# Seeding a product's PSUM bank with ScalarE, and one down word earlier, in a two-layer macaron encoder

## The chip, the cores and the metric

The kernel runs on one core of one Trainium2 chip. TensorE multiplies, ScalarE, VectorE and GpSimd work on tiles beside it, SyncE issues most of the loads from HBM. The metric is the device time of one execution in microseconds (us), the median of three runs. A profile of one further execution shows every instruction of every engine.

## The reference

The input x has 256 tokens of 1024 features, all in float32. Two layers each do three steps, and each step ends in a layer norm of the old x, scaled, plus the step's result: a SwiGLU feed-forward, a mixer (layer 0 a bidirectional mLSTM, layer 1 a windowed attention), and a second SwiGLU feed-forward. What this change touches is the feed-forward, which is done four times:

```python
gu = x @ w_in                          # (256, 1024) @ (1024, 5632)
g, u = gu[..., :2816], gu[..., 2816:]
return (silu(g) * u) @ w_out           # (256, 2816) @ (2816, 1024)
```

## The kernel before, in words

**Three matmuls for one.** A float32 product is computed to nearly full precision by splitting each operand into a high part (rounded to the type that TensorE takes in one pass) and a low part (what the rounding left). `mm3` (line 617) then issues high by high, high by low and low by high into the same PSUM bank. ScalarE casts the high part, VectorE subtracts to get the low part. This holds for weights (tiles `w_raw`, `s_raw` to `w_hi`, `w_lo`), for x (`xT_hi`, `xT_lo`) and for the hidden activations (`h_hi`, `h_lo`). A piece of weights of 128 x 1024 is called a word.

**A feed-forward** (`ffn`, line 770). Its 2816 hidden columns are done as 512 plain columns, 256 plain columns and four blocks of 512. Each of the four blocks is one call of `seven` (line 946): it gets the four 128-token by 512-column results (two token tiles t, gate and up) with seven products in place of eight, a Strassen-Winograd scheme over sums of weights and sums of x (`S1` to `S4`). One call of `product` (line 930) takes two words and issues 12 matmuls of 512 columns.

**Order of work in a block.** The products go to PSUM banks qa, qb and qc, of a ring of four banks `pw` that `wbank` gives out; each product's follow-up on the other engines is a function `end1` to `end7` that is issued right behind it. In issue order:

1. product 1 into qa; `end1` (line 955) has ScalarE copy qa to an SBUF tile `e` (the page calls all these temporaries `e` or `g`).
2. `before()`: for the first block it transposes the 256 plain columns (`turn`, line 1033); for the second to fourth block it is `second` (line 1002) of the block before, which transposes that block's result for token tile 1 with `tr` (line 790): four TensorE transposes into one bank, ScalarE casts the bank to `h_hi`, VectorE subtracts to `h_lo` (`split_evac`, line 636).
3. product 2 into qc; `end2` (line 958) asks VectorE to add qc onto `e`. The sum is the gate of token tile 0.
4. `down(1)` (line 914): one word of w_out times one 128-column chunk of the hidden activations, added onto the four `py` banks of the output. For each token tile it issues six matmuls, tile 0 first, then tile 1. Chunks are taken in order: the first block's first `down` reads chunk 2 of the plain columns; the first `down` of the second, third and fourth block reads chunk 6, 10 and 14, which is the first chunk of the block before. Its token tile 0 was transposed near the end of that block (`end4`, line 977), its token tile 1 by the `second` of step 2. The order of h in `mm3` is high, high, low: the third matmul of each three loads `h_lo`.
5. products with S1 (into qb; `end5` copies it) and S2 (onto qa; `end6` copies it and has ScalarE do the SiLU of `e` in place), a second `down`, products with S3 and S4, and so on. The first three blocks do four `down`, the last block two; six more follow in `tail`.

**What sets the order on the other engines.** All engines execute their own instructions in the order in which they were issued. The kernel writes that order with a planner of its own: class `Paced` (line 65) keeps a clock for TensorE, VectorE and ScalarE while the program is written out, adding a cost for each instruction (`on_tensor`, line 162). After every matmul or transpose, `Weights.fill` (line 376) hands ScalarE another cast of a weight word (`high`, line 300) if ScalarE's clock is less than 300 ns ahead of TensorE's, and VectorE a subtraction (`low`, line 324), a sum of weights (`sum`) or a deferred follow-up (`when_ready`, line 365), by the same rule. `flush` (line 372) issues all deferred follow-ups at once; `down` calls it first. The words are listed in `plan` in the order in which the products use them (`seven` at line 492 of the planning code), and loads follow that list; a ring of ten split words lies between the splitting and TensorE.

Of the kernel before, what the change touches and what calls it, by code (L numbers as in the profile page):

```python
# [11 lines left out]
AF = mybir.ActivationFunctionType  # L12
# [52 lines left out]
class Paced:  # L65
# [94 lines left out]
            self.mark(o, self.act + 125)  # L160

    def on_tensor(self, name, n, out, ins):
        self.pe = max(self.pe, self.when(*ins)) + (109.0 if name == "transpose" else n / 2.4 + 13.3)
        for o in out:
            self.mark(o, self.pe + 200)
        if self.filler is not None:
            self.filler()
# [277 lines left out]
def trunk_kernel(ctx: ExitStack, tc: tile.TileContext, x, ffn_w_in, ffn_w_out, ln_g, ln_b, ml_w_in, ml_gate_b,  # L445
                 ml_norm_g, ml_w_out, at_w_in, at_sink, at_w_out, out):
    nc = Paced(tc.nc)
# [12 lines left out]
    def word(src, k, tag="w_raw"):  # L460
        words.append(dict(src=src, k=k, tag=tag))
        return len(words) - 1
# [3 lines left out]
    def split_of(w, scale=None, needs=None, takes=2720.0, behind=0.0):  # L466

        plan.append(dict(word=w, k=words[w]["k"], scale=scale, needs=needs, due=clock[0], behind=behind))
        clock[0] += takes
        return len(plan) - 1  # L470

    def piece(src, k, scale=None, takes=2720.0):
        split_of(word(src, k), scale, None, takes)

    def two(w, r0, c0):
        return w[r0:r0 + 256, c0:c0 + 512].rearrange("(k p) f -> p k f", p=128)
# [12 lines left out]
    def rows(w, c, scale=None):  # L489
        piece(w[c * 128:(c + 1) * 128, :].rearrange("(k p) f -> p k f", p=128), 1, scale)  # L490

    def seven(w, c0, c1, n, down):

        def at(r0, c):
            return [two(w, r0 + 256 * j, c) for j in range(2)]

        b12, b11, b22 = ([word(x, 2, TAGS[r]) for x in at(*p)]
                         for r, p in ((2, (0, c1)), (4 if n % 2 else 1, (0, c0)), (3, (512, c1))))
        b21 = at(512, c0)
        full = n < SEVENS - 1  # L500
        half = 1360.0
        s1 = [split_of(w_, None, None, half) for w_ in b11]
        for j in range(2):
            after[s1[j]] = [(b11[j], b12[j]), (b12[j], at(512, c1)[j])]
        for a in b21:
            piece(a, 2, None, half)
        down(1)
        t1 = [split_of(w_, None, p, half, BY_SUM) for w_, p in zip(b11, s1)]
        for j in range(2):
            after[t1[j]] = [(b11[j], b22[j])]  # L510
        t2 = [split_of(w_, None, p, half, BY_SUM) for w_, p in zip(b11, t1)]
        for j in range(2):
            after[t2[j]] = [(b11[j], b21[j])]
        down(1)
        for w_, p in zip(b12, s1):
            split_of(w_, None, p, half, BY_MOVE)
        for w_ in b22:
            split_of(w_, None, None, half)
        if full:
            down(1)  # L520
        for w_, p in zip(b11, t2):
            split_of(w_, None, p, half, BY_MOVE)
        if full:
            down(1)

    ends = {}
    for j, (kind, l, i, _) in enumerate(stages):
        if kind == "ffn":
# [3 lines left out]
            def down(n):  # L532
                for _ in range(n):
                    rows(wo, next(nth))
# [48 lines left out]
    W = Weights(nc, wpool, rooms, words, plan, after)  # L583
# [9 lines left out]
    ident = consts.tile([128, 128], F32, name="ident")  # L593
# [2 lines left out]
    nc.vector.tensor_scalar(ident, ji, 0.0, None, op0=OP.is_equal)  # L596
    mhalf = consts.tile([128, 2], F32, name="mhalf")
    nc.gpsimd.memset(mhalf, -0.5)

    gcol = consts.tile([128, 8], F32, name="gcol")  # L600
    gw = consts.tile([128, 8, 16], F32, name="gw")
# [20 lines left out]
    def pair(p, *idx):  # L622
        return p[0][idx], p[1][idx]

    def wbank(shape=(128, 512)):
        return psum.tile(list(shape), F32, name="pw", tag="pw", bufs=4)

    def ybank(shape=(128, 512)):
        return psum.tile(list(shape), F32, name="py", tag="py", bufs=4)
# [3 lines left out]
    def tok(t):  # L633
        return slice(t * 128, (t + 1) * 128)
# [135 lines left out]
    def ffn(l, i, n, pending, last):  # L770
        with ExitStack() as ph:
# [7 lines left out]
            def temp(name):  # L779
                return pool.tile([128, 512], F32, name=name, tag="t", bufs=6)  # L780

            start = pending is None
# [7 lines left out]
            def tr(hB, t, h):  # L790
                p = wbank((128, 4, 128))
                for k in range(4):
                    nc.tensor.transpose(p[:, k], h[:, k * 128:(k + 1) * 128], ident)
                split_evac(pair(hB, A, A, tok(t)), p, wait=True)

            def chunks(hB, n_):
                c0 = len(hT)
                for c in range(n_):
                    hT[c0 + c] = pair(hB, A, c)
# [114 lines left out]
            def down(n_):  # L914
                if not y:
                    y.extend([ybank() for _ in range(2)] for _ in range(2))
                W.flush()
                for _ in range(n_):
                    c = done_[0]
                    w, = W.take(1)  # L920
                    for t in range(2):
                        for o in range(2):
                            mm3(y[t][o], pair(hT[c], A, tok(t)), pair(w, A, 0, slice(o * 512, o * 512 + 512)),
                                c == 0, False)
                    W.done()
                    done_[0] += 1
# [3 lines left out]
            def product(bank, x_of, first, then):  # L930

                for j in range(2):
                    w, = W.take(1)
                    for k in range(2):
                        mm3(bank, x_of(2 * j + k), pair(w, A, k), first and j == k == 0, j == k == 1, not first)
                then()
                W.done()

            def copied(bank, name):
                e = temp(name)  # L940
                nc.scalar.copy(e, bank)
                return e
# [3 lines left out]
            def seven(full, before):  # L946

                of = lambda k0, t: (lambda k: pair(xT, A, k0 + k, tok(t)))
                sum_ = lambda name: (lambda k: pair(xs[name], A, k))
                v = {}  # L950
                hB = h_room(4)
                chunks(hB, 4)
                qa, qc = wbank(), wbank()

                def end1():
                    v["g0"] = copied(qa, "e1")

                def end2():
                    W.when_ready(lambda: nc.vector.tensor_add(v["g0"], v["g0"], qc), qc)

                def end5():
                    v["u1"] = copied(qb, "e5")

                def end6():
                    v["u0"] = copied(qa, "e2")
                    W.flush()
                    nc.scalar.activation(v["g0"], v["g0"], AF.Silu)

                def end7():
                    W.when_ready(lambda: nc.vector.tensor_sub(v["u1"], v["u1"], qa), qa)  # L970

                def end3():
                    W.flush()
                    W.when_ready(lambda: nc.vector.tensor_sub(v["u0"], qb, v["u0"]), qb)
                    W.when_ready(lambda: nc.vector.tensor_mul(v["u0"], v["g0"], v["u0"]))

                def end4():
                    v["g1"] = temp("g1")
                    nc.scalar.activation(v["g1"], qa, AF.Silu)
                    W.flush()  # L980
                    tr(hB, 0, v["u0"])
                    W.when_ready(lambda: nc.vector.tensor_mul(v["u1"], v["g1"], v["u1"]), v["g1"])

                product(qa, of(0, 0), True, end1)
                before()
                if not full:
                    gb.extend(load_ln(lambda name: W.room(name, TAGS[1]), l, n))
                product(qc, of(4, 0), True, end2)
                down(1)
                qb = wbank()  # L990
                product(qb, sum_("S1"), True, end5)
                product(qa, sum_("S2"), False, end6)
                down(1)
                product(qa, sum_("S3"), False, end7)
                product(qb, sum_("S4"), False, end3)
                if full:
                    down(1)
                product(qa, of(4, 1), False, end4)
                if full:
                    down(1)  # L1000

                def second():
                    W.flush()
                    tr(hB, 1, v["u1"])

                return second
# [16 lines left out]
            hh = []  # L1023
# [9 lines left out]
            def turn():  # L1033
                p = wbank((128, 2, S))
                for t in range(2):
                    for k in range(2):
                        nc.tensor.transpose(p[:, k, tok(t)], hh[t][:, k * 128:(k + 1) * 128], ident)
                split_evac(hp, p, wait=True)

            down(1)  # L1040
# [595 lines left out]
```

## Time and profile before

| what | value |
|---|---|
| runs | 914.19, 912.9 and 914.21 us, median 914.19 us |
| the profiled execution | span 911.7 us from its first to its last instruction; no time of its own is given beside the span |
| granted TensorE clock | 0.999 |
| TensorE matmuls | 902.5 us busy, 4459 instructions |
| VectorE | 804.4 us busy, 971 instructions |
| ScalarE | 573.1 us busy, 793 instructions |
| GpSimd | 152.5 us busy, 192 instructions |
| HBM read | 206.65 MB |

The page lists the engines as PE (TensorE's matmuls), PEld (its weight loads, which overlap with the matmuls), DVE (VectorE), ACT (ScalarE) and POOL (GpSimd). A row of a group reads: line, engine, operation, output <- inputs, shapes, count, then the busy time in us and the mean ns of one. Nearly all instructions bear line 180, since a wrapper there records them, so they are told apart by their tiles. A row of the timeline reads: start in us, duration in us, engine, operation, and in square brackets how long the engine had been idle before it and on whom it waited. Successive instructions of one engine can overlap by some 0.1 us in the rows, since a row ends when the result is written and the next one has started by then. Matmul rows overlap more (a row of 0.39 us every 0.23 us).

### The profile page before, as it was taken

What the parts mean: (1) busy time and instruction counts of PE and PEld (TensorE: products, weight loads), DVE (VectorE), ACT (ScalarE), POOL (GpSimd) and SP (SyncE); (2) the same over time, 40 slices, a digit from 0 to 9 for tenths busy, and PEclk for the clock granted to TensorE, in tenths of its full rate; (3) what the DMA queues carried; (4) which work ended last, traced back from release to release, by engine and by line L of the source; (5) the groups of instructions that cost most, each with busy time, mean ns of one, the idle gap of its engine ahead of it and who ended that gap; (6) DMA issues with size and microseconds to landing.
All of it is one profiled execution on the core that took longest, in us unless ns stands there. A gap on an engine that the chain in (4) does not pass through costs nothing.

```text
span 911.7 us, 12563 instructions
## 1 busy us (share of the span) xinstructions
PE 902.5 (99%) x4459; PEld 757.4 (83%) x4459; DVE 804.4 (88%) x971; ACT 573.1 (63%) x793; POOL 152.5 (17%) x192
## 2 busy tenths in 40 slices
PE   9999999999999999999999999999999999999996
PEld 7888888889988888888888888888898888888885
DVE  5999999886799898999888899998869889899886
ACT  5776777356664656776646676764569566676660
POOL 0111123113211011212011111110425301111110
PEclk9999999999999999999999999999999999999999
DMA  8999998546637898997868989986534587899851
GB/s 281 367 328 259 288 274 215 162 137 186 208 111 246 296 234 244 290 285 234 241 193 269 259 257 283 272 223 197 159 119 140 163 293 221 204 298 278 252 138 47
DMA packets 100703, 208.53 MB, mean 229 GB/s; under 512 B 6904, under 2 KB 21264, under 8 KB 100640
## 3 DMA queue, kind: packets, MB, share of 16 engines
q1 hardware_dynamic: 82368, 173.04, 54.2%
q0 software_dynamic: 17696, 33.65, 22.3%
q10 hardware_dynamic: 576, 1.05, 0.3%
q8 instruction: 35, 0.57, 0.3%
q14 instruction: 28, 0.23, 0.1%
HBM read 206.65 MB, written 1.05 MB: 228 GB/s over the span
## 4 chain that ended last, share of the span: by engine, by line
PE 98%; DVE 1%; DMA 0%; issue 0%; DVEq 0%
PE pw L180 64%; PE py L180 35%; DMA x<-in_x_dram 0%; DVE x L180 0%; DVE stats L180 0%; DVEq L1632 0%; DVE mv L180 0%; DVE rs L180 0%
## 5 line engine op out<-in xcount | busy, mean ns | idle before, releaser
L180 DVE TENSOR_TENSOR w_lo<-w_raw,w_hi 128x1024 fp32r<-128x1024 f32 (+1 forms) x213 | 255.2, 1219 | 26.6 <-ACT w_hi L180 24.8
L180 ACT CAST w_hi<-w_raw 128x1024 fp32r<-128x1024 f32 (+1 forms) x213 | 218.9, 1049 | 80.3 <-PE py L180 21.7
L180 DVE TENSOR_TENSOR w_lo<-s_raw,w_hi 128x1024 fp32r<-128x1024 f32 x192 | 228.6, 1219 | 18.3 <-ACT w_hi L180 18.2
L180 ACT CAST w_hi<-s_raw 128x1024 fp32r<-128x1024 f32 x192 | 196.6, 1054 | 58.4 <-PE py L180 23.3
L180 PE MATMUL pw<-w_hi,xT_hi 128*128 128x512 f32 x480 | 189.5, 396 | 0.0
L180 PE MATMUL pw<-w_hi,xT_lo 128*128 128x512 f32 x480 | 187.0, 391 | 0.0
L180 PE MATMUL pw<-w_lo,xT_hi 128*128 128x512 f32 x480 | 186.7, 390 | 0.0
L122 POOL DMA_DIRECT2D s_raw<-in_ffn_w_in_dram x64 | 77.4, 1211 | 484.1 <-DVE s_raw L180 226.3
L180 PE MATMUL py<-w_hi,h_hi 128*128 128x512 f32 x349 | 138.2, 396 | 0.0
L180 PE MATMUL py<-w_hi,h_lo 128*128 128x512 f32 x349 | 136.2, 390 | 0.0
L180 PE MATMUL py<-w_lo,h_hi 128*128 128x512 f32 x349 | 136.0, 390 | 0.0
L180 PEld LDWEIGHTS pw<-w_hi,xT_lo 128*128 128x128 f32 x480 | 90.0, 188 | 19.1
L180 PEld LDWEIGHTS pw<-w_lo,xT_hi 128*128 128x128 f32 x480 | 90.3, 188 | 18.6 <-DVE w_lo L180 1.2
L180 PEld LDWEIGHTS pw<-w_hi,xT_hi 128*128 128x128 f32 x480 | 90.1, 188 | 17.4 <-ACT w_hi L180 0.2
L180 PE MATMUL pw<-w_hi,S_hi 128*128 128x512 f32 x256 | 99.7, 390 | 0.0
L180 PE MATMUL pw<-w_lo,S_hi 128*128 128x512 f32 x256 | 99.7, 389 | 0.0
L180 PE MATMUL pw<-w_hi,S_lo 128*128 128x512 f32 x256 | 99.7, 389 | 0.0
L180 PEld LDWEIGHTS py<-w_hi,h_lo 128*128 128x128 f32 x349 | 65.5, 188 | 14.1
L180 DVE TENSOR_TENSOR s_raw<-s_raw,s_raw 128x1024 f32<-128x1024 f32 x64 | 76.8, 1219 | 0.3
L180 PEld LDWEIGHTS py<-w_lo,h_hi 128*128 128x128 f32 x349 | 65.7, 188 | 13.0
L180 PEld LDWEIGHTS py<-w_hi,h_hi 128*128 128x128 f32 x349 | 65.6, 188 | 12.7
L180 PEld LDWEIGHTS pw<-w_hi,S_lo 128*128 128x128 f32 x256 | 48.1, 188 | 10.0
(205 smaller groups left out, 1122.7 us busy)
## 6 DMA issues: line engine op xcount, KB each, us to landing
s_raw<-in_ffn_w_in_dram SPq DMA_DIRECT2D x96, 512.0 KB, 8.0
w_raw<-in_ffn_w_out_dram SPq DMA_DIRECT2D x88, 512.0 KB, 6.1
w_raw<-in_ffn_w_in_dram SPq DMA_DIRECT2D x64, 512.0 KB, 5.7
s_raw<-in_ffn_w_in_dram POOLq DMA_DIRECT2D x64, 512.0 KB, 8.3
w_raw<-in_ml_w_in_dram SPq DMA_DIRECT2D x24, 512.0 KB, 4.6
w_raw<-in_ffn_w_in_dram SPq DMA_DIRECT2D x32, 256.0 KB, 6.0
w_raw<-in_at_w_in_dram SPq DMA_DIRECT2D x12, 512.0 KB, 4.8
w_raw<-in_ml_w_out_dram SPq DMA_DIRECT2D x8, 512.0 KB, 4.1
```

The costliest lines, as they stand in the source:

```text
L122: self.nc.gpsimd.dma_start(ap, source, accum_op=OP.add)
L180: r = f(out, *args, **kw)
```

## The change

In each of the sixteen blocks, ScalarE's copy of product 1 goes into qc, the PSUM bank of product 2, and product 2 accumulates on it (`first` is now False). VectorE's addition in `end2` goes away. The SiLU of the gate reads qc and is issued in `end5`, one product earlier than before. The first `down` of each block moves from behind product 2 to ahead of it, and the word list moves its word with it. A matmul that is to add onto what another engine wrote needs the bank's accumulation marks to be set, so the transposes into `pw` banks in `tr` and `turn` no longer each start a new accumulation: only the first of the four does (`turn_in`). The planner's cost of a transpose is chosen by the width of the output, 128, as the transposes now come as matmuls.

```diff
     def on_tensor(self, name, n, out, ins):
-        self.pe = max(self.pe, self.when(*ins)) + (109.0 if name == "transpose" else n / 2.4 + 13.3)
+        self.pe = max(self.pe, self.when(*ins)) + (109.0 if n == 128 else n / 2.4 + 13.3)
...
             after[s1[j]] = [(b11[j], b12[j]), (b12[j], at(512, c1)[j])]
+        down(1)
         for a in b21:
             piece(a, 2, None, half)
-        down(1)
...
+    def turn_in(o, a, k):
+        nc.tensor.matmul(o, a, ident, is_transpose=True, start=k == 0, stop=True, skip_group_check=k > 0)
...
             def tr(hB, t, h):
                 p = wbank((128, 4, 128))
                 for k in range(4):
-                    nc.tensor.transpose(p[:, k], h[:, k * 128:(k + 1) * 128], ident)
+                    turn_in(p[:, k], h[:, k * 128:(k + 1) * 128], k)
                 split_evac(pair(hB, A, A, tok(t)), p, wait=True)
...
                 def end1():
-                    v["g0"] = copied(qa, "e1")
+                    nc.scalar.copy(qc, qa)
 
                 def end2():
-                    W.when_ready(lambda: nc.vector.tensor_add(v["g0"], v["g0"], qc), qc)
+                    pass
 
                 def end5():
+                    v["g0"] = temp("g0")
+                    nc.scalar.activation(v["g0"], qc, AF.Silu)
                     v["u1"] = copied(qb, "e5")
 
                 def end6():
                     v["u0"] = copied(qa, "e2")
                     W.flush()
-                    nc.scalar.activation(v["g0"], v["g0"], AF.Silu)
...
                 before()
                 if not full:
                     gb.extend(load_ln(lambda name: W.room(name, TAGS[1]), l, n))
-                product(qc, of(4, 0), True, end2)
                 down(1)
+                product(qc, of(4, 0), False, end2)
                 qb = wbank()
...
                     for k in range(2):
-                        nc.tensor.transpose(p[:, k, tok(t)], hh[t][:, k * 128:(k + 1) * 128], ident)
+                        turn_in(p[:, k, tok(t)], hh[t][:, k * 128:(k + 1) * 128], 2 * t + k)
                 split_evac(hp, p, wait=True)
```

## The prediction

> **What bounds the kernel now.** I read the page first, then TensorE's own waits, then the chain of waits in order of time, then the windows.
>
> ```profile
> span 911.7 us, 12563 instructions
> PE 902.5 (99%) x4459; PEld 757.4 (83%) x4459; DVE 804.4 (88%) x971; ACT 573.1 (63%) x793; POOL 152.5 (17%) x192
> PE 98%; DVE 1%; DMA 0%; issue 0%; DVEq 0%
> ```
> ```profile
> PE py L180 <- DVE ident L180: 1.7, 1, 1.7
> PE py L180 <- DMA x<-in_x_dram: 0.4, 1, 0.4
> ```
> ```profile
> 84.83 2.72 PE py L180 x12
> 87.55 5.44 PE pw L180 x24
> ```
> ```profile
> 358.00:449.00 91.00, 91.00 (x416) 75.36 (x416) 87.68 (x87) 64.26 (x76) 12.05 (x10) 1.00 0.93 265
> ```
>
> The chain of what ended last is 98% TensorE. Its waits, the second fence, are all of them: 2.1 us, both before the first block. So a busy TensorE here is not one that hides waits in overlapping rows. The chain's rows confirm it: 24 matmuls in 5.44 us and 12 in 2.72 us are both 0.2267 us each. In a window that holds a feed-forward's last three blocks and a bit more, TensorE is busy 91.00 of 91.00 us, at full granted clock, and VectorE 87.68 us. TensorE has no slack, and the others have little enough that it matters when they deliver.
>
> Two things follow. The change takes no matmul and no transpose away, so it has next to nothing to win. And every stretch in which TensorE has to wait for something new is added to the time in full.
>
> **The change part by part.** First the pieces that leave TensorE's queue alone.
>
> ```profile
> L180 ACT COPY e<-pw 128x512 f32<-128x512 f32 x48 | 28.2, 587 | 40.3 <-PE pw L180 39.9
> L180 ACT ACTIVATE e<-e 128x512 f32<-128x512 f32 x16 | 10.1, 634 | 0.0
> L180 ACT ACTIVATE g<-pw 128x512 f32<-128x512 f32 x16 | 9.6, 600 | 28.7 <-PE pw L180 28.7
> L180 DVE TENSOR_TENSOR e<-e,pw 128x512 f32<-128x512 f32 x32 | 21.8, 680 | 0.0
> ```
>
> *The addition.* Sixteen of the 32 additions `e<-e,pw` go: 16 x 0.68 = 10.9 us of VectorE. TensorE never waits for VectorE in a block, so this is worth 0. *The SiLU* reads PSUM instead of SBUF: 600 ns for 634, off the path, 0. It stands one product earlier on ScalarE, which delays the copy of the S1 product by about 0.5 us; that copy is used two products later, 0. *The copy* itself now writes PSUM, which no row of ScalarE shows. Bounds are the copy out of PSUM, 587 ns, and the activation without PSUM on either side, 634; a gain like the one on the reading side (34 ns) isn't excluded, so from 553 to 634. I take 587. *Transposes*: same instruction, same count, 0. *The planner's price*: 128-wide transposes cost it 109 as before; only the four 64-wide transposes of the mLSTM fall to 40, which moves its clock by 0.28 us once, 0.
>
> *The new wait of product 2 for the copy.* The next fences show one place; the copy ends at 82.27, product 2 will start 12 matmuls behind the transposes, at 81.84 + 2.72 = 84.56. The moved `down` hides it with 2.3 us to spare, two casts' worth; without the `down` it would cost 0.4 us per block. *The moved word:* one load of 512 KB on SyncE's queue passes two of 512 KB, and its cast and subtraction pass theirs. Splitting runs words ahead; the subtraction at 80.38 below is the last of these three words before 84.67, where the old `down` needs it. In the new order it is the second word of product 2, needed 1.36 us later: 0.
>
> Now the piece that matters. `down` now stands right behind the transposes of `second`, and it reads what they produce.
>
> ```profile
> 81.48 0.60 PE L180 MATMUL pw<-ident,e 128*128 128x128 f32 x4
> 81.84 0.47 PE L180 MATMUL pw<-w_hi,xT_hi 128*128 128x512 f32 x1
> 82.15 0.39 PE L180 MATMUL pw<-w_lo,xT_hi 128*128 128x512 f32 x1
> ...
> 84.67 0.39 PE L180 MATMUL py<-w_hi,h_hi 128*128 128x512 f32 x1
> ```
> ```profile
> 75.92 0.19 PEld L180 LDWEIGHTS py<-w_hi,h_hi 128*128 128x128 f32 x1
> 76.03 0.19 PEld L180 LDWEIGHTS py<-w_lo,h_hi 128*128 128x128 f32 x1
> ```
> ```profile
> 81.68 0.59 ACT L180 COPY e<-pw 128x512 f32<-128x512 f32 x1 [1.21 <-PE pw L180]
> 82.16 1.05 ACT L180 CAST w_hi<-s_raw 128x1024 fp32r<-128x1024 f32 x1
> 83.11 0.59 ACT L180 CAST h_hi<-pw 128x512 fp32r<-128x512 f32 x1
> ```
> ```profile
> 80.38 1.22 DVE L180 TENSOR_TENSOR w_lo<-w_raw,w_hi 128x1024 fp32r<-128x1024 f32 x1
> 81.51 2.36 DVE L180 TENSOR_TENSOR w_lo<-s_raw,w_hi 128x1024 fp32r<-128x1024 f32 x2
> 83.78 0.69 DVE L180 TENSOR_TENSOR h_lo<-pw,h_hi 128x512 fp32r<-128x512 f32 x1
> ```
>
> Count from the transposes, T = 81.48. Before, product 2 lay between them and the `down` at T + 3.19. After, `down` starts at once. Six matmuls of token tile 0 come first; their chunk is old. The second matmul behind the transposes stands at T + 0.67, so the seventh, the first of tile 1, is due at 0.67 + 5 x 0.2267 = T + 1.80, and the ninth, which loads `h_lo`, at T + 2.26. A weight load that has nothing to hide behind leads its matmul by 0.11 us (75.92 to 76.03), so `h_lo` must be there at T + 2.15.
>
> When is it there? ScalarE does the copy, then a cast of a weight word, then `h_hi`, which ends at T + 2.22 (83.70). `flush` in `down` now puts the subtraction next on VectorE: of the two subtractions at 81.51 the second goes behind it. It starts 0.04 us after `h_hi` (row below), takes 0.69, and another 0.04 to TensorE: T + 2.99. **TensorE waits 0.84 us.** Four more matmuls of this `down` and product 2 stand behind it in the queue, so nothing fills the gap. VectorE idles about 1.1 us at the head of its queue for `h_hi`; behind it is a word that the S1 product needs at 87.39 or later, 2 us after, so 0 more.
>
> The weight cast between copy and `h_hi` decides this. Where it fell ahead of the copy, there is no stall:
>
> ```profile
> 111.39 1.05 ACT L180 CAST w_hi<-s_raw 128x1024 fp32r<-128x1024 f32 x1 [1.78 <-DVE s_raw L180]
> 112.56 0.59 ACT L180 COPY e<-pw 128x512 f32<-128x512 f32 x1
> 113.04 0.59 ACT L180 CAST h_hi<-pw 128x512 fp32r<-128x512 f32 x1
> ```
> ```profile
> 112.35 1.22 DVE L180 TENSOR_TENSOR w_lo<-w_raw,w_hi 128x1024 fp32r<-128x1024 f32 x1
> 113.48 1.22 DVE L180 TENSOR_TENSOR w_lo<-s_raw,w_hi 128x1024 fp32r<-128x1024 f32 x1
> 114.62 0.68 DVE L180 TENSOR_TENSOR h_lo<-pw,h_hi 128x512 fp32r<-128x512 f32 x1
> ```
>
> Here the copy again starts 0.20 after T (112.36), `h_hi` ends at T + 1.27, VectorE is free by then, `h_lo` is there at T + 2.04, in time by 0.11 us. The 0.04 us from the end of one engine's row to the start of the engine that waits for it come from a transpose near the end of a block, and I use them for TensorE too:
>
> ```profile
> 107.12 0.58 ACT L180 CAST h_hi<-pw 128x512 fp32r<-128x512 f32 x1
> ```
> ```profile
> 107.74 0.69 DVE L180 TENSOR_TENSOR h_lo<-pw,h_hi 128x512 fp32r<-128x512 f32 x1 [0.27 <-ACT h_hi L180]
> ```
>
> There are twelve such places: blocks two to four of four feed-forwards; a first block's `down` reads chunk 2, long done. I went through all of them. Five have the cast in between, the one above first and this one last, with the same 2.02 us from the copy's start to the end of `h_hi`:
>
> ```profile
> 834.19 0.59 ACT L180 COPY e<-pw 128x512 f32<-128x512 f32 x1 [0.96 <-PE pw L180]
> 834.67 1.05 ACT L180 CAST w_hi<-s_raw 128x1024 fp32r<-128x1024 f32 x1
> 835.62 0.59 ACT L180 CAST h_hi<-pw 128x512 fp32r<-128x512 f32 x1
> ```
>
> Three are free like the one at 112.36. The other four have a late sum of weights, so VectorE or the copy is late. Two of these come out at the edge, in time to within 0.1 us, and count as 0. The remaining two:
>
> ```profile
> 539.91 0.38 PE L180 MATMUL pw<-ident,e 128*128 128x128 f32 x2
> ```
> ```profile
> 542.34 1.22 DVE L180 TENSOR_TENSOR w_lo<-s_raw,w_hi 128x1024 fp32r<-128x1024 f32 x1
> ```
> ```profile
> 803.11 0.38 PE L180 MATMUL pw<-ident,e 128*128 128x128 f32 x2
> ```
> ```profile
> 804.84 1.22 DVE L180 TENSOR_TENSOR w_lo<-s_raw,w_hi 128x1024 fp32r<-128x1024 f32 x1
> ```
>
> In each, `h_lo` would take the place of the subtraction shown: 542.34 + 0.69 + 0.04 = 543.07 against 539.91 + 2.15 = 542.06, 1.01 us; 804.84 + 0.72 = 805.56 against 805.26, 0.30 us.
>
> The sum is 5 x 0.84 + 1.01 + 0.30 = **5.5 us**. The span would be 917.2. The median of the runs lies 2.5 us above the span of the profile, for what lies around it, so I predict 914.2 + 5.5 = 919.7 us. The unknown length of the copy is on this path in the five places: 5 x (-0.034 to +0.047), from -0.2 to +0.2 us.
>
> The Trainium skill bears on that copy in "Perfetto Trace Analysis", Optimizing Scalar/DVE Operations: an access costs ScalarE about 93 ns in SBUF and 51 in PSUM. The two SiLU rows, 634 and 600 ns, agree for reading; for writing no row of before shows it. By it the copy would be some 40 ns shorter and the sum, as an estimate, 5.3 us.
>
> **The rivals.**
>
> *The chain fits, no stall.* If the planner in its new rhythm puts no cast between copy and `h_hi`, all places look like 112.36 and the time stays 914.2. For it: three of twelve do now and two nearly. Against: the planner casts when ScalarE's clock is under 300 ns ahead; what kept it out at 112.36 was a cast held up by a late sum on VectorE, and with 0.68 us less per block VectorE will be late less often. It decides at 0.11 us: any cast, 0.95 us, in between breaks it. Chance 22%.
>
> *Every place stalls, or VectorE is behind too.* With the cast in all twelve: 12 x 0.84 = 10.1 us, 924.3. If also one more subtraction, 1.13 us (112.35 to 113.48), gets in ahead of `h_lo` each time: 12 x 1.97 = 23.6 us, 937.8. Against the latter: `flush` puts `h_lo` right behind `h_hi`'s issue. Chance 20%.
>
> *Something else is late*, a word whose order was swapped or a subtraction behind VectorE's new idle stretch: one cast and one subtraction, 2.3 us, in some of sixteen blocks, 3 to 15 us on top of the time before. Chance 4%.
>
> *Faster.* VectorE at 87.68 of 91 us might hold things up in a way that the waits don't show, and 10.9 us less of it would help. But TensorE is at 91.00 of 91.00; all of its idle time is 911.7 - 902.5 = 9.2 us, in the start and behind the last matmul, where no block is. Only cheaper transposes could win: the 44 groups of four that go through `tr` and `turn` would have to shrink by 10 ns in each transpose, of 110 ((82.15 - 81.48 - 0.2267) / 4), for 0.2%. The time would be some 912. Chance 4%. The Trainium skill, same page and section, would have one move work to ScalarE when VectorE is saturated. It doesn't say that the engine relieved must be the one that is waited for; the waits speak against a gain here.
>
> **How the numbers follow.** My forecast, four to nine places with a stall, 3.4 to 7.6 us more, 917.6 to 921.8 us, has 50%. A measurement of this kernel can tell about 0.2%, 1.8 us, from no change. Slower by more than that: 50 + 20 + 4 = 74%; within it: 22%; faster: 4%. The range takes in most of the no-stall case, below 914.2, and all twelve places with a little more: 913.4 to 927. It leaves out faster, a few in a hundred of no stall, and the half of the second rival where VectorE is behind as well.
>
> **What would show it.** In the profile after, TensorE's waits should list `py` waiting for ACT `h_hi` or DVE `h_lo`, 5 to 12 times, up to about 1 us each, all right behind `pw<-ident,e` in blocks two to four. VectorE's waits for `h_hi` should grow from what they are now:
>
> ```profile
> DVE h_lo L180 <- ACT h_hi L180: 12.1, 7, 2.4
> ```
>
> No wait of `pw` for the copy should appear. If TensorE has no waits and the time is the same, the first rival holds. If waits for `w_lo` or `w_hi` appear, the third.

## The result, and the profile after

The changed kernel takes 923.41 us in the median of four runs (923.18 to 923.82); the kernel before took 913.78 us in four runs beside it. The ratio is 1.0108 [1.0094, 1.0123], 9.6 us slower. The forecast was 919.7 us, 5.5 us slower, with twelve stalls (924.3 us) as a rival. The profiled execution took 923.82 us, 922.1 of it in the span, 10.4 us more than the span before.

The head of the page after, and then all waits of TensorE's matmuls:

```profile
span 922.1 us, 12531 instructions
PE 910.0 (99%) x4459; PEld 756.7 (82%) x4459; DVE 797.1 (86%) x955; ACT 579.5 (63%) x793; POOL 152.9 (17%) x192
```
```profile
PE py L180 <- ACT h_hi L180: 3.4, 12, 0.3
PE py L180 <- DVE ident L180: 1.7, 1, 1.7
```

TensorE is still 99% busy, and with the same 4459 matmuls it is busy for 7.5 us more. That is no more work. A matmul that starts late gets a longer row (0.50 us for 0.39), and rows overlap, so most of a short stall is counted as busy. What tells is the first row of the second fence, new and there twelve times. Its 3.4 us are only what the overlap leaves uncovered. The waits of the weight loads show more of it:

```profile
PEld py L180 <- ACT h_hi L180: 8.6, 12, 0.7
...
PEld py L180 <- DVE h_lo L180: 5.1, 12, 0.4
```

The window with three of the places reads alike. It is 4 us longer than the one shown of before, so that it takes in the same three places:

```profile
358.00:453.00 95.00, 94.14 (x421) 76.05 (x420) 86.84 (x85) 65.98 (x75) 12.09 (x10) 1.00 0.90 249
```

TensorE was busy 91.00 of 91.00 us; now 0.86 us are uncovered, 0.29 at each of the three places. The starts of the matmuls give the whole price. Here is the first place on TensorE's timeline, with the transposes at T = 81.79:

```profile
81.79 0.60 PE L180 MATMUL pw<-ident,e 128*128 128x128 f32 x4
82.15 0.47 PE L180 MATMUL py<-w_hi,h_hi 128*128 128x512 f32 x1
...
83.15 0.39 PE L180 MATMUL py<-w_lo,h_hi 128*128 128x512 f32 x1
83.38 0.40 PE L180 MATMUL py<-w_hi,h_lo 128*128 128x512 f32 x1
84.06 0.50 PE L180 MATMUL py<-w_hi,h_hi 128*128 128x512 f32 x1 [0.29 <-ACT h_hi L180]
84.40 0.40 PE L180 MATMUL py<-w_lo,h_hi 128*128 128x512 f32 x1
84.79 0.50 PE L180 MATMUL py<-w_hi,h_lo 128*128 128x512 f32 x1
85.13 0.39 PE L180 MATMUL py<-w_hi,h_hi 128*128 128x512 f32 x1
```

Starts follow each other by 0.2267 us when nothing is late. The matmul at 84.06 comes 0.68 us after the one ahead of it, the next ones 0.34, 0.39 and 0.34. What exceeds the pitch is 0.45 (the wait for `h_hi`), 0.11, 0.16 (the wait for `h_lo`) and 0.11: **0.83 us**. ScalarE and VectorE at the same place:

```profile
81.99 0.57 ACT L180 COPY pw<-pw 128x512 f32<-128x512 f32 x1 [1.25 <-PE pw L180]
82.47 1.05 ACT L180 CAST w_hi<-s_raw 128x1024 fp32r<-128x1024 f32 x1
83.42 0.59 ACT L180 CAST h_hi<-pw 128x512 fp32r<-128x512 f32 x1
```
```profile
84.04 0.69 DVE L180 TENSOR_TENSOR h_lo<-pw,h_hi 128x512 fp32r<-128x512 f32 x1 [1.04 <-ACT h_hi L180]
84.65 1.22 DVE L180 TENSOR_TENSOR w_lo<-s_raw,w_hi 128x1024 fp32r<-128x1024 f32 x1
```

A weight cast lies between the copy and `h_hi`, and `h_hi` ends 2.22 us after T. All twelve places look like this, so the stalls take 12 x 0.83 = 10.0 of the 10.4 us of span. The rest is there ahead of any block: in the start, a matmul that stood at 14.07 us before stands at 14.40 now. The chain that ended last can be followed back to 812.77 us, and at each of the three places in that stretch it crosses the other engines; this is the last one:

```profile
871.90 2.74 PE pw L180 x12
874.64 0.02 issue
874.66 0.46 ACT pw L180
875.12 0.02 issue
875.15 1.05 ACT w_hi L180
876.20 0.49 ACT h_hi L180
876.69 0.04 issue
876.74 1.92 PE py L180 x6
```

Read downwards: product 1, ScalarE's copy of it (0.46), a weight cast that nobody here waits for (1.05), `h_hi` (0.49), then the six matmuls of token tile 1. The cast is on the path only by its place in ScalarE's order. VectorE's other work does not hold up `h_lo` here: at 84.04 the engine had been idle for 1.04 us, waiting for `h_hi`.

### The profile page after: what moved, and what is told of

Its sections match the earlier page's. It is cut to its first block, busy times and chain, and to the rows that moved or that the text cites. A ratio compares the mean times of both kernels' runs of the same rounds, so it can differ in the third digit from the quotient of the medians.

```text
span 922.1 us, 12531 instructions
## 1 busy us (share of the span) xinstructions
PE 910.0 (99%) x4459; PEld 756.7 (82%) x4459; DVE 797.1 (86%) x955; ACT 579.5 (63%) x793; POOL 152.9 (17%) x192
## 3 DMA queue, kind: packets, MB, share of 16 engines
q10 hardware_dynamic: 576, 1.05, 0.3%
HBM read 206.65 MB, written 1.05 MB: 225 GB/s over the span
## 5 line engine op out<-in xcount | busy, mean ns | idle before, releaser
L180 ACT CAST w_hi<-s_raw 128x1024 fp32r<-128x1024 f32 x192 | 200.9, 1054 | 62.8 <-PE py L180 36.5
L180 PE MATMUL py<-w_hi,h_hi 128*128 128x512 f32 x349 | 141.0, 404 | 3.4 <-ACT h_hi L180 3.4
L180 PEld LDWEIGHTS pw<-w_lo,S_hi 128*128 128x128 f32 x256 | 48.1, 188 | 10.0
```

Source lines behind the costliest of these rows:

```text
L180: r = f(out, *args, **kw)
```

## The experiments

In each profile I counted at how many of the twelve places a weight cast stands between ScalarE's copy of product 1 and `h_hi`, and at how many TensorE's matmuls wait for `h_hi` or `h_lo`. Each ratio is to runs of the kernel before that were made beside those of the row. A median within 0.2% of before is called the same.

| kernel | median, us | ratio to before | cast in between | `py` waits for `h` |
|---|---|---|---|---|
| after | 923.41 | 1.0108 [1.0094, 1.0123] | 12 | 12 |
| move_only | 921.66 | 1.0085 [1.007, 1.01] | 9 | 10 |
| seed_only | 920.93 | 1.0076 [1.0059, 1.0093] | 12 | 0 |
| no_cast | 914.83 | 1.001 [1.0, 1.0019] | 0 | 1 |
| half_down | 913.36 | 0.9995 [0.9986, 1.0005] | 12 | 0 |
| low_last | 920.58 | 1.007 [1.0054, 1.0087] | 12 | 12 |
| extra_copy | 927.29 | 1.0142 [1.0127, 1.0158] | 12 | 12 |
| silu_back | 921.69 | 1.0083 [1.0068, 1.0098] | 9 | 9 |
| early_silu | 914.61 | 1.0008 [0.9998, 1.0018] | 12 | 1 |
| turn_only | 912.91 | 0.9994 [0.9984, 1.0003] | 5 | 0 |
| add_kept | 923.74 | 1.0109 [1.0094, 1.0124] | 12 | 12 |
| no_add | 912.95 | 0.9993 [0.9984, 1.0002] | 5 | 0 |

The theory: the moved `down` reads an `h_hi` and `h_lo` that a weight cast holds up. The rivals: that the copy into PSUM costs the time by itself, that the queue of words suffers from the new order, or that the new transposes are dearer.

### The moved down alone, and the seed alone

**move_only**, from the kernel before: only the word and the issue of `down(1)` move.

```diff
+        down(1)
         for a in b21:
             piece(a, 2, None, half)
-        down(1)
...
+                down(1)
                 product(qc, of(4, 0), True, end2)
-                down(1)
```

> The kernel before with the first down word of each block moved ahead of product 2, in the word list and in the issue order; the copy to SBUF, the addition and the late SiLU stay. My theory: the loss comes from the move alone, through the wait of the down for h_hi and h_lo, so it is slower than before by 0.84 us for each place where a weight cast stands between the copy and h_hi; with nine of twelve such places in the planner's order for this kernel, and up to 1 us in each of the other three, 913.8 + 7.6 to 10 = 921.4 to 924. The rival that the saved addition makes casts come early (the reason given in the prediction) puts the count back to about five to seven: 918 to 920. The rival that accumulating onto a bank written by ScalarE costs the time: 914.

It took 921.66 us, 8.0 more than the 913.7 of before beside it. TensorE's waits:

```profile
PE py L180 <- ACT h_hi L180: 2.7, 10, 0.3
```

Ten stalls in 8.0 us, 0.8 us each. Nine of them stand where a cast is in between. At the tenth, T = 544.38, the cast stands ahead of the copy, but it had to wait for a late sum of weights on VectorE; so the copy starts only 1.07 us after T, and `h_hi` is late all the same. It is one of the two places that the prediction charged for such a sum. So the moved `down` stalls without any copy into PSUM, and the number of stalls is nearer to the twelve of after than to the five that I had counted in the trace of before.

**seed_only**, from the kernel after: word and issue of `down` go back behind product 2.

```diff
         for a in b21:
             piece(a, 2, None, half)
+        down(1)
...
-                down(1)
                 product(qc, of(4, 0), False, end2)
+                down(1)
```

> The kernel after with the down word back behind product 2. My theory: no wait for h_hi or h_lo, but product 2 now stands right behind the transposes and waits for the copy into its bank, which ends 0.77 us after the transposes begin, while product 2 could start at 0.36 to 0.44: 0.35 to 0.55 us in each of sixteen blocks, 5.6 to 8.8 us, 919.4 to 922.6. The rival that accumulation onto a written bank is itself slow: 923 or more. If TensorE doesn't have to wait for the copy: 914.

It took 920.93 us. TensorE's waits, matmuls first and weight loads second, say where:

```profile
PE pw L180 <- ACT pw L180: 3.6, 16, 0.2
```
```profile
PEld pw L180 <- ACT pw L180: 7.4, 16, 0.5
```

Without the `down` ahead of it, product 2 waits for the copy in all sixteen blocks, 7.4 / 16 = 0.46 us each, and the span shows nearly all of it (918.8 against 911.7, 7.1 us). The move is needed to cover the copy, and it costs more than it covers: 16 x 0.46 against 12 x 0.83 us. The two don't add up, since only one of the two pieces of work can stand right behind the transposes.

### The cast out of the way

**no_cast**, from the kernel after: no weight cast or subtraction is handed out between the end of product 1 and the end of `before()`. They follow a little later; none is left out.

```diff
                 def end1():
                     nc.scalar.copy(qc, qa)
+                    W.fill = nc.filler = lambda: None
...
                 before()
+                del W.fill
+                nc.filler = W.fill
```

> The kernel after, with the planner's filling switched off from the end of product 1 to the end of the transposes in each block, so that no weight cast can stand between the copy and h_hi. My theory: h_hi ends at 1.27 us after the start of the transposes and h_lo at 2.0, in time by 0.1 us; the stalls go and the time is that of before, 913.8 to 914.5. If the stall has another cause than that cast (the copy into PSUM, the bank, the moved word's own weights): 920 to 923.4.

It took 914.83 us, 1.1 more than before and 8.6 less than after. ScalarE at the first place:

```profile
81.31 0.57 ACT L180 COPY pw<-pw 128x512 f32<-128x512 f32 x1 [1.22 <-PE pw L180]
81.79 0.59 ACT L180 CAST h_hi<-pw 128x512 fp32r<-128x512 f32 x1
82.27 2.01 ACT L180 CAST w_hi<-s_raw 128x1024 fp32r<-128x1024 f32 x2
```

The cast now comes behind `h_hi`. At eleven places no matmul waits; the one wait that is left is, on TensorE's timeline,

```profile
541.91 0.39 PE L180 MATMUL py<-w_lo,h_hi 128*128 128x512 f32 x1
542.81 0.50 PE L180 MATMUL py<-w_hi,h_lo 128*128 128x512 f32 x1 [0.52 <-DVE h_lo L180]
```

0.90 - 0.23 = 0.67 us late. It is the same place as the tenth of move_only: here `h_lo` starts almost 1 us after `h_hi` has ended, since VectorE is behind. With the cast away the rest of the change, copy into PSUM, transposes and word order together, is worth 0 to within that one stall and the measurement.

### The same words, the down in two halves

**half_down**, from the kernel after: the six matmuls of token tile 0 stay ahead of product 2, the six of tile 1 go behind it. The planner's order of words is that of after.

```diff
-                down(1)
-                product(qc, of(4, 0), False, end2)
...
+                w, = W.take(1)
+                for t in range(2):
+                    for o in range(2):
+                        mm3(y[t][o], pair(hT[c], A, tok(t)), pair(w, A, 0, slice(o * 512, o * 512 + 512)), c == 0, False)
+                    if t == 0:
+                        for j in range(2):
+                            p, = W.take(1)
+                            for k in range(2):
+                                mm3(qc, of(4, 0)(2 * j + k), pair(p, A, k), False, j == k == 1, True)
+                        end2()
+                        W.done(i)
...
```

> The kernel after, with the early down cut in two: its six matmuls of token tile 0 ahead of product 2, its six of token tile 1 behind. Copy and h_lo are both covered then. My theory: no stall at all, 913.8 to 914.5, and nothing gained over before since TensorE is full there. If VectorE's saved additions are worth anything by themselves, less than 912.

It took 913.36 us, 0.9995 [0.9986, 1.0005]: the same as before, with the cast still in between at all twelve places, and these waits of TensorE's matmuls, none of them in a block:

```profile
PE py L180 <- DVE ident L180: 1.7, 1, 1.7
PE py L180 <- DMA x<-in_x_dram: 0.3, 1, 0.3
```

Six matmuls, 1.36 us, cover the copy, and tile 1 gets product 2's 2.72 us more. So the cast costs nothing where nobody waits for `h_hi` so early, and neither the order of words nor the seed costs anything.

### The size of the wait

**low_last**, from the kernel after: in the first `down`, tile 1 issues its high by high and low weight by high h first and the products with `h_lo` last.

```diff
-                down(1)
+                down(1, True)
...
+                        for a, b in ((0, 0), (0, 1), (1, 0)):
+                            for o in range(2):
+                                nc.tensor.matmul(y[1][o], h[a], w[b][:, 0, o * 512:o * 512 + 512], start=False, stop=False)
```

> The kernel after, with the six matmuls of token tile 1 in the early down in another order: the four that load h_hi first, the two that load h_lo last. My theory cuts the stall of 0.84 us into a part for h_hi and a part for h_lo: in the trace of after 0.45 + 0.11 us before and behind the first matmul of tile 1, and 0.16 + 0.11 at the first that loads h_lo. Two more matmuls, 0.45 us, now lie ahead of h_lo, so its part goes and that for h_hi stays: 12 x 0.56 = 6.7 us over before, 920.5 (919.8 to 921). If the stall is one wait for h_lo alone, 0.45 us go and 923.4 - 5.4 = 918. If the order within the down doesn't matter: 923.4.

It took 920.58 us, 2.8 less than after. The row of weight loads waiting for `h_lo` is gone and the other is unchanged:

```profile
PEld py L180 <- ACT h_hi L180: 8.6, 12, 0.7
```

The stall is made of two: 12 x (0.16 + 0.11) = 3.2 us for `h_lo`, nearly all saved here, and 12 x (0.45 + 0.11) = 6.7 us for `h_hi`, left (measured: 7.0 over before).

**extra_copy**, from the kernel after: one more short ScalarE copy ahead of `h_hi` in each `second` (`late` is true there alone).

```diff
+                if late:
+                    nc.nc.scalar.copy(pool.tile([128, 256], F32, name="spare", tag="spare", bufs=1), h[:, 0:256])
                 split_evac(pair(hB, A, A, tok(t)), p, wait=True)
```

> The kernel after with one more copy on ScalarE, 128x256 from SBUF to SBUF into a spare tile, right ahead of h_hi in the twelve places; the planner's clock doesn't know of it. My theory: all that ScalarE does ahead of h_hi there is on the path, so each place is later by the time that ScalarE takes for it, 0.27 to 0.38 us: 3.2 to 4.6 us more than after, 926.6 to 928. If ScalarE is not on the path: 923.4.

It took 927.29 us, 3.9 more than after. The group of the new copy, and TensorE's wait:

```profile
L798 ACT COPY spare<-e 128x256 f32<-128x256 f32 x16 | 6.5, 407 | 1.4 <-DVE e L180 1.4
```
```profile
PE py L180 <- ACT h_hi L180: 7.0, 12, 0.6
```

The copy takes 0.41 us, some 0.1 of it overlapped; the wait grew by (7.0 - 3.4) / 12 = 0.30 us at each place, and 12 x 0.30 = 3.6 of the 3.9 us. Four of the sixteen copies stand where nobody waits. So what delays `h_hi` on ScalarE goes into the time one for one at the twelve places.

### Why twelve

The prediction took five casts from the trace of before. What changed the number?

**silu_back**, from the kernel after: the SiLU goes back behind `end6`'s copy.

```diff
                 def end5():
-                    v["g0"] = temp("g0")
-                    nc.scalar.activation(v["g0"], qc, AF.Silu)
                     v["u1"] = copied(qb, "e5")
...
                     W.flush()
+                    v["g0"] = temp("g0")
+                    nc.scalar.activation(v["g0"], qc, AF.Silu)
```

> The kernel after with the SiLU of the gate issued one product later, in end6, where it was before (it still reads the PSUM bank). Theory now: whether a cast falls between copy and h_hi is set by the planner's rhythm on ScalarE, and the earlier SiLU, not the saved addition, turned nine such places into twelve. So nine places stall in full, the other three by up to 1 us: 921.4 to 924, with three fewer waits of 0.84 us than after, if those three have none 920.9. By the saved addition as the cause: twelve again, 923.4.

It took 921.69 us, with nine stalls:

```profile
PE py L180 <- ACT h_hi L180: 2.6, 9, 0.3
```

At the other three places the cast stands ahead of the copy, as at 112.36 in the trace of before. So the early SiLU brings three of the stalls, and not all of the difference to five.

**early_silu**, from the kernel before: only the SiLU moves up, into `end5`, with a `flush` ahead of it so that the addition comes first.

```diff
                 def end5():
+                    W.flush()
+                    nc.scalar.activation(v["g0"], v["g0"], AF.Silu)
                     v["u1"] = copied(qb, "e5")
...
                     W.flush()
-                    nc.scalar.activation(v["g0"], v["g0"], AF.Silu)
```

> The kernel before with the SiLU of the gate issued one product earlier, in end5, behind a flush so that the addition stands ahead of it; nothing else. Theory: the cast falls between copy and h_hi in all twelve places, though VectorE has as many additions as before; product 2 still covers h_hi and h_lo, so the time doesn't change: 913.8. By the saved addition as the cause of twelve: five places as before. Either way no time is lost, if the moved down is the only thing that makes the place costly.

It took 914.61 us, the same as before. But its ScalarE rows at the first place (T = 82.17) have the order of after, and so do all twelve:

```profile
82.37 0.59 ACT L180 COPY e<-pw 128x512 f32<-128x512 f32 x1 [1.23 <-PE pw L180]
82.85 1.05 ACT L180 CAST w_hi<-s_raw 128x1024 fp32r<-128x1024 f32 x1
83.80 0.59 ACT L180 CAST h_hi<-pw 128x512 fp32r<-128x512 f32 x1
```

Moving the SiLU up by one product, with VectorE's addition and the order of words as before, is enough for twelve casts. With the `down` where it was, eleven of them cost nothing. At the twelfth, T = 805.05, a late sum holds up the copy by 1.09 us more; the `down` behind product 2 then starts its third matmul of tile 1 0.42 us late, on `h_lo`.

**turn_only**, from the kernel before: only `turn_in` in `tr` and `turn`, and the planner's cost line.

```diff
-                    nc.tensor.transpose(p[:, k], h[:, k * 128:(k + 1) * 128], ident)
+                    turn_in(p[:, k], h[:, k * 128:(k + 1) * 128], k)
...
```

> The kernel before with the transposes of the hidden activations issued as in the change (only the first of four starts a new accumulation) and with the planner's price by width; nothing else. Both theories: 913.8, same as before. A time above 915.6 would say that the marks of the bank or the planner's line have a price.

It took 912.91 us, the same, with five casts in between. The transposes that don't restart an accumulation cost and gain nothing.

**add_kept**, from the kernel after: VectorE again does an addition with qc in each block, in two halves, into a spare that nobody reads.

```diff
                 def end2():
-                    pass
+                    e = pool.tile([128, 256], F32, name="spare", tag="spare", bufs=1)
+                    for s_ in (slice(0, 256), slice(256, 512)):
+                        W.when_ready(lambda s_=s_: nc.vector.tensor_add(e, xt[0][:, s_], qc[:, s_]), qc)
```

> The kernel after with VectorE's work put back: behind product 2 it adds two halves of 256 columns of that bank onto parts of x into a spare tile that nobody reads, 0.7 us per block. Theory now (rhythm of ScalarE, set by the earlier SiLU): twelve places as in after, 923.4. The reason given in the prediction (VectorE less late makes casts come early): five to nine places, 918 to 921.4.

It took 923.74 us, as after. VectorE's load and the stalls:

```profile
PE 909.4 (99%) x4459; PEld 755.3 (82%) x4459; DVE 809.2 (88%) x987; ACT 580.0 (63%) x793; POOL 152.3 (17%) x192
```
```profile
PE py L180 <- ACT h_hi L180: 3.4, 12, 0.3
```

VectorE is busier by 12.1 us than after and by 4.8 than before, and there are twelve stalls all the same.

**no_add**, from the kernel before: `end2` does nothing. The kernel leaves the addition out, so the gate lacks product 2.

```diff
                 def end2():
-                    W.when_ready(lambda: nc.vector.tensor_add(v["g0"], v["g0"], qc), qc)
+                    pass
```

> The kernel before without VectorE's addition of product 2 to the gate; it leaves that addition out, so product 2 is computed and not used. Theory: TensorE never waits for it, so 10.9 us less work on VectorE change nothing: 913.8, and five places with the cast in between as before. If a busy VectorE holds TensorE up in a way that the waits don't show: less than 912.

It took 912.95 us, 0.9993 [0.9984, 1.0002], the same as before, with five casts in between:

```profile
PE 902.4 (99%) x4459; PEld 757.5 (83%) x4459; DVE 795.8 (87%) x955; ACT 573.8 (63%) x793; POOL 152.0 (17%) x192
```

So 8.6 us less on VectorE neither win time nor alter the number of casts.

What goes with the casts is VectorE's order. These are its rows ahead of a free place of before (T = 112.36) and ahead of the same place in early_silu (T = 113.05), where a cast stands in between:

```profile
108.34 0.68 DVE L180 TENSOR_TENSOR e<-g,e 128x512 f32<-128x512 f32 x1
108.94 1.22 DVE L180 TENSOR_TENSOR w_lo<-s_raw,w_hi 128x1024 fp32r<-128x1024 f32 x1
110.08 2.35 DVE L180 TENSOR_TENSOR s_raw<-s_raw,s_raw 128x1024 f32<-128x1024 f32 x2
```
```profile
109.32 0.68 DVE L180 TENSOR_TENSOR e<-g,e 128x512 f32<-128x512 f32 x1
109.92 2.36 DVE L180 TENSOR_TENSOR s_raw<-s_raw,s_raw 128x1024 f32<-128x1024 f32 x2
```

In before one weight subtraction stands ahead of the two sums. They end at T + 0.07, the cast that needs them waits, and it comes out just ahead of the copy. In early_silu the subtraction is not there, the sums end at T - 0.77, that cast is done before T, and the next one stands between the copy and `h_hi`. In the traces of all kernels but no_cast, 144 places, exactly one subtraction stands there at each of the 27 without a cast in between, and none (89) or two (28) at each of the 117 with one. That is a match in the rows, not an experiment.

## Why the prediction was right, and where it was not

**What bounds the kernel: right.** TensorE had no slack, and a new wait on it went into the time in full: 12 x 0.83 us in a span that grew by 10.4.

**The saved addition is worth 0: right.** no_add shows it alone (VectorE's busy time falls by 8.6 us there, not by the predicted 10.9). The Trainium skill, "Perfetto Trace Analysis", Optimizing Scalar/DVE Operations, says that offloading work to ScalarE may make sense if VectorE is saturated. Here VectorE was busy for 88% of the span, and by no_add's time there was nothing to win by relieving it. Nor did the work go to ScalarE, which has 793 instructions in both kernels: the sum is now formed by product 2's accumulation.

**The copy, the transposes, the planner's price and the swapped words at 0: right.** half_down holds all four and takes the time of before; turn_only holds the transposes and the price alone. The range of 553 to 634 ns for the copy held, at 570 ns (row below), and its 0.4 us per block without the `down` came out at 0.46 in seed_only.

**The place and price of a stall: right in sum, not in its parts.** Predicted were 0.84 us, all of it in the ninth matmul, the first that needs `h_lo`. Measured were 0.83, most of it two matmuls earlier: `h_hi` is late as well, and the seventh matmul meets it first. Both numbers stood in the prediction, `h_hi` at T + 2.22 and the seventh matmul due at T + 1.80, and were not compared. The sum had to agree, as the last of the two waits, for `h_lo`, sets when the queue goes on. low_last shows that the two parts can be told apart.

**The count of places: wrong.** This is the step that failed: "Five have the cast in between", read off the trace of before and carried over, with 1.01 and 0.30 us for two more. All twelve had it, and the two late places became like the others. With the count of twelve the sum is the rival's 10.1 us, against 9.6 measured. So the forecast of four to nine places, which had 50%, missed, and what came is the first half of the second rival; the range held because it took in that case.

The reason that the prediction gave for more casts, "VectorE will be late less often", does not hold. At the free places the sums on VectorE do end late, but lateness alone does not keep a cast out: in early_silu at T = 805.05 they end at T + 1.38, and a cast stands in between all the same. Nor does the load of VectorE decide: with the addition gone and nothing else changed there are five (no_add), with that work put back and all else changed there are twelve (add_kept). What moves the number is the order in which the planner issues: nine with the moved `down` and its word (move_only, and silu_back where the addition is gone), twelve with the SiLU one product earlier (early_silu, after, seed_only). Why in the planner an earlier SiLU or a moved word changes what VectorE is given ahead of the sums was not traced and stays open.

**The signs to look for: right.** Waits of `py` for `h_hi` came twelve times, at the upper end of five to twelve, and twelve for `h_lo` in the rows of the weight loads; no `pw` waits for the copy; VectorE's wait for `h_hi`, 12.1 us in seven before, is now

```profile
DVE h_lo L180 <- ACT h_hi L180: 26.3, 22, 2.4
```

**The time around the span: 2.5 us taken, 1.7 found.** Wherever a run's time and span are both on record, the time is 1.7 us longer (923.82 and 922.1 here; from 1.66 to 1.79 in the others). The 2.5 us came from setting a span against the median of other executions: the one that was profiled before, 911.7 us of span, will have taken some 913.4 us, 0.4 less than the median of 913.78, and the one after took 0.4 more than its median. This is why 10.4 us of span are 9.6 us of time.

## What to carry to other kernels

Where the busiest engine never waits, ask of each moved piece which operand it reads that was made just ahead, and follow that operand's chain on the other engines with everything that can be queued into it; relief of an engine that nobody waits for is worth nothing. If a planner decides what is queued there, the order in the trace of before is not the order after: price the case in which the filler lands in the gap every time, or hold the filler off. Cover for a short new wait need not be a whole step: the six matmuls whose operands were long done covered the copy by themselves, and the six behind them brought the stall.

## What the runs showed of the hardware

The groups of ScalarE's copies in the profile after, one into PSUM and one into SBUF:

```profile
L180 ACT COPY e<-pw 128x512 f32<-128x512 f32 x32 | 18.8, 588 | 21.7 <-PE pw L180 21.7
...
L180 ACT COPY pw<-pw 128x512 f32<-128x512 f32 x16 | 9.1, 570 | 21.9 <-PE pw L180 21.9
```

The row of the write to PSUM is 18 ns shorter. It brings nothing here: the next instruction starts 0.48 us after the copy in both kernels (81.99 to 82.47, and 81.68 to 82.16 before). The Trainium skill, "Perfetto Trace Analysis", Optimizing Scalar/DVE Operations, gives its two access figures, 42 ns apart, as engine-busy times and not as lengths of rows, so the distance between starts is what to hold against them. By it this write saves nothing. The reading side agrees: in the trace of before the next instruction starts at the earliest 0.53 us after a SiLU of an SBUF tile and 0.49 after one of a PSUM bank.

A short stall of TensorE has a second part. The matmul behind the one that waited starts 0.34 us after it, not 0.2267 (84.06 to 84.40, 84.79 to 85.13). The prediction put these 0.11 us, as the lead of an uncovered weight load, ahead of the late matmul (the rows it read, 75.92 and 76.03, are two weight loads in succession). Here `h_lo` ends at 84.04 + 0.69 = 84.73, and the row of the matmul that needs it starts 0.06 us later; the 0.11 us come behind it. Two short waits in a row cost 0.22 us for that alone, 2.6 us over the twelve places.
